# A GLU in five passes, Newton steps on GpSimd, and residual rows asked for ahead in a one-core YOCO decoder step

## The chip, the cores and the metric

The kernel runs on one core of one Trainium2 chip. The metric is the device time of one execution in microseconds; the median of three runs of the kernel before is 2706.2 us (2705.61 to 2708.99).

The core has TensorE (PE: matmuls and transposes into PSUM), VectorE (DVE) and ScalarE (ACT) for elementwise work, GpSimd (POOL), and SyncE (SP), whose queue issues nearly all DMAs here. Each engine takes its instructions in order.

## What is computed

A prompt of 1024 tokens and a sample batch of 8 x 8 tokens go through two layers of width 1024. Layer 0 is an S5 state-space mixer with a gated output (GLU) and a convolutional feed-forward network (FFN); layer 1 is differential attention and another FFN. What the change touches, in the reference's words:

```python
z = jax.nn.gelu(y)
gl = z @ w_glu                                   # 1024 -> 2048
out = gl[..., :D_MODEL] * jax.nn.sigmoid(gl[..., D_MODEL:])
x = x + rmsnorm(out, a_post_g)                   # end of the GLU: post norm and residual
h = rmsnorm(x, f_pre_g) @ w_up                   # FFN, up: 1024 -> 5632
f_out = (gelu(gate) * val) @ w_down              # after a 3-tap convolution; down: 2816 -> 1024
x = x + rmsnorm(f_out, f_post_g)                 # end of each FFN
```

Layer 1's attention ends in the same way: `x = x + rmsnorm(o @ w_o, b_post_g)`, and its FFN follows.

## The kernel before

Tokens lie in nine tiles: eight of 128 prompt tokens (0 to 7) and one of 64 sample tokens (number 8, NTT). Activations that a matmul reads stand transposed in SBUF as a rounded part `xh` and a remainder `xl`; a product is three matmuls (`mm3`, L805 to L807), for the sample tile two (L979, L980).

**GLU** (`glu`). The 2048 output columns are done in four passes `q`, each with 256 value columns and their 256 gate columns, over all nine tiles in `ORDER_U`. For each pass `glu_units(q)` loads four weight units of 512 KB and splits them into two parts (ScalarE L788, VectorE L789). A tile's pass is 24 matmuls of 512 columns (`tok_mm`), a sigmoid on ScalarE (L1042) and a product on VectorE (L1043) into 256 columns of the tile's row buffer `ao[tt]`. In the last pass each tile is finished by `tail.add`.

**Tails.** `tail_a` loads the residual rows (L845, into one of two buffers `xr`), takes the sum of squares on ScalarE (`square_sum`, L820), multiplies by the post gain (VectorE, L849), turns the mean square into 1/rms (`rstd_from`: two set-up instructions and three Newton steps of two 128x1 instructions each, L126 and L130), adds the residual (L852) and stores the rows (L853). `tail_n` does the norm of the next layer in the same way (L862). `tail_b` transposes the result (TensorE L868) and splits it into `xh` and `xl` (L140 on ScalarE, L141 on VectorE). `Combos.pair` does so for the tile pairs (0,3), (1,4), (2,5), and forms differences (L909 to L912) for a Strassen-like product in the up-projection. `Tail` keeps tiles that are normed but not yet transposed in a list; beyond `lag` of them the oldest is transposed. `lag` is 2 in the GLU and 1 in the output projection.

**Output projection** (`o_proj`). Column half 1 of the nine tiles is done in `ORDER_O`; the five tiles of `EARLY` (NTT, 0, 3, 1, 4), whose other half was computed during attention, are finished there. The four of `LATE` (2, 5, 6, 7) only give half 1 to DRAM (`yod`), with its share of the sum of squares (`part`), and are finished in a pass of their own over half 0.

**FFN.** `ffn_up` loops over 22 column pairs; each ends in a store of a gated row block to DRAM (`gd`, L1191). `ffn_down` takes the 22 blocks in chunks, adds partial products in `acc` (L1404), and calls `done(tt)` for each tile after the last chunk; in layer 1 that is `tail_a` alone, whose result is the kernel's output. A sample tile's two halves are first added through a buffer `xr` (L1370, L1371).

**Buffers.** `slot(tag)` hands out shared buffers: 14 of `acc` (row buffers, gains, combos), 5 of `gr` (512 columns), 2 of `xr`; weights come into 2 buffers `raw` and are split into 11 rotating ones. A planner orders the instructions of all engines for the whole program by priority (program order) and its own model of durations; on the chip each engine then keeps that order.

Of the kernel before, what the change touches and what calls it, by code (L numbers as in the profile page):

```python
# [10 lines left out]
F32 = mybir.dt.float32  # L11
# [62 lines left out]
def trunk_kernel(ctx, tc, I, O):  # L74
# [7 lines left out]
    def nm(s):  # L82
        uid[0] += 1
        return f"{s}_{uid[0]}"
# [23 lines left out]
    def flat(t, n=512):  # L108
        return t[:, 0:n]

    def rstd_from(pool, ss, n, parts, tag, n_mean=D, bufs=None, pre=None):


        kw = {"bufs": bufs} if bufs else {}
        v = pool.tile([P, n], F32, tag=tag + "v", name=nm("rv"), **kw)
        s = pool.tile([P, n], F32, tag=tag + "s", name=nm("rs"), **kw)
        r = pool.tile([P, n], F32, tag=tag + "r", name=nm("rr"), **kw)
        p = slice(0, parts)
        if pre is None:
            V.tensor_scalar(v[p], ss, -0.5 / n_mean, -0.5 * EPS, op0=ALU.mult, op1=ALU.add)  # L120
        else:
            V.scalar_tensor_tensor(v[p], ss, -0.5 / n_mean, pre, op0=ALU.mult, op1=ALU.add)
        V.tensor_scalar(r[p].bitcast(I32), v[p].bitcast(I32), -0.5, RSQ_MAGIC, op0=ALU.mult, op1=ALU.add)
        for _ in range(3):
            if n == 1:
                V.scalar_tensor_tensor(s[p], r[p], r[p], v[p], op0=ALU.mult, op1=ALU.mult)  # L126
            else:
                V.tensor_tensor(s[p], r[p], r[p], ALU.mult)
                V.tensor_tensor(s[p], s[p], v[p], ALU.mult)
            V.scalar_tensor_tensor(r[p], s[p], 1.5, r[p], op0=ALU.add, op1=ALU.mult)  # L130
        return r
# [677 lines left out]
    def tokens(tt):  # L809
        return (tt * P, P) if tt < NTT else (SEQ, TS)  # L810
# [12 lines left out]
    def rms_rstd(t, n):  # L823
        return rstd_from(pools["ph"], square_sum(t, n), 1, n, "n1", bufs=4)

    sums = {}

    def part(y, tt, post, cs):
# [8 lines left out]
            V.tensor_scalar(p, ss, -0.5 / D, -0.5 * EPS, op0=ALU.mult, op1=ALU.add)  # L837
        V.tensor_tensor(y, y, post[0:n, cs], ALU.mult)

    def tail_a(y, tt, post, xsrc, xdst, last=False, rest=slice(0, D)):  # L840


        t0, n = tokens(tt)
        xr = slot("xr")
        nc.sync.dma_start(xr[0:n], xsrc(tt))  # L845
        halves = (slice(512, D), slice(0, 512)) if last else (slice(0, D),)
        ss = square_sum(y[:, rest], n)
        for hs in halves if last else (rest,):
            V.tensor_tensor(y[:, hs], y[:, hs], post[0:n, hs], ALU.mult)  # L849
        r = rstd_from(pools["ph"], ss, 1, n, "n1", bufs=4, pre=sums.pop(tt, None))  # L850
# [4 lines left out]
    def tail_n(y, tt, gain=None):  # L855

        n = tokens(tt)[1]
        r = rms_rstd(y, n)
# [59 lines left out]
    class Tail:  # L918
# [6 lines left out]
        def add(self, y, tt, *a, **kw):  # L925
            tail_a(y, tt, *a, **kw)
            self.norm()
            self.n.append((y, tt))
            if len(self.q) > self.lag:
                self.pop()  # L930

        def norm(self):
            for a in self.n:
                tail_n(*a, self.gain)
            self.q += self.n
            self.n = []

        def pop(self):
# [74 lines left out]
    def glu(ws):  # L1013

        zt = slot("acc")[0:TS, 0:D]
        zv = zt.rearrange("r (b g c) -> r b g c", g=8, c=16)
        for u in range(3):
            for j in range(min(3, 8 - 3 * u)):
                zs = zsd.rearrange("(b u) r w -> u r b w", u=3)[u, 32 * j : 32 * j + NB]
                nc.sync.dma_start(zv[:, :, 3 * u + j], zs.rearrange("s b (t c) -> (s t) b c", c=16))  # L1020
        post = row_bcast(I["a_post_g"][0])
        tail.gain = row_bcast(I["f_pre_g"][0])
        ao = {}
        for q in range(4):
            if q:
                ws = glu_units(q)
            qs_ = slice(q * 256, (q + 1) * 256)
            for tt in ORDER_U:
                n = tokens(tt)[1]
                if q == 0:  # L1030
                    ao[tt] = slot("acc")
                    if tt == ORDER_U[4]:
                        tail_b(zt, NTT)
                        xsx = sample_pair()
# [6 lines left out]
                sg = slot("gr")  # L1041
                A.activation(sg[0:n, 0:256], g[:, 256:512], AF.Sigmoid)  # L1042
                V.tensor_tensor(ao[tt][0:n, qs_], g[:, 0:256], sg[0:n, 0:256], ALU.mult)  # L1043
                if q == 3:
                    if tt == 0:
                        tail.combos = Combos()
                    y = ao[tt][0:n, 0:D]
                    tail.add(y, tt, post, x_in, x_scr(x1d))
            if q == 0:
                conv_params(0)  # L1050
                lam_column(cpool)
        tail.norm()
# [305 lines left out]
            self.upto(1)  # L1358

    def ffn_down(dn, i, xsrc, xdst, norm):  # L1360
        acc = {}
        post = [None]
        nch = len(dn.plan)

        def done(tt):
            n = tokens(tt)[1]
            y = acc[tt][0:n, 0:D]
            if n < P:
                u = slot("xr")
                A.copy(u[0:n], acc[tt][n : 2 * n, 0:D])  # L1370
                V.tensor_tensor(y, y, u[0:n], ALU.add)  # L1371
            if norm:
                tail.add(y, tt, post[0], xsrc, xdst)
            else:
                tail_a(y, tt, post[0], xsrc, xdst, tt == NTT - 1)

        def plain(k, c, tt):
            kind, f0, nf = dn.plan[c]
# [93 lines left out]
        for k, (c, tt) in enumerate(dn.steps):  # L1472
            kind, f0, nf = dn.plan[c]
            if c == nch - 1 and post[0] is None:
                post[0] = row_bcast(I["f_post_g"][i])
            if kind == "p":
                dn.upto(k + 2)
                plain(k, c, tt)
# [486 lines left out]
    def o_proj():  # L1965
# [7 lines left out]
        for half, tts in ((1, ORDER_O), (0, LATE)):  # L1973
# [4 lines left out]
            for tt in tts:  # L1978
# [15 lines left out]
                else:  # L1994
                    fold_sample(yh, ps)
                if end:
                    tail.add(y, tt, post, x_scr(x2d), x_scr(x3d), rest=hs)
                else:
                    part(yh, tt, post, hs)
                    nc.sync.dma_start(yod[t0 : t0 + n], yh)  # L2000
                    tail.norm()
                    tail.pop()
# [2 lines left out]
    dtile = lambda name, shape: dpool.tile(shape, F32, tag=name, name=name)  # L2005
    x2d = dtile("x2d", [T, D])
    gd = dtile("gd", [NF, P, TG])
    x3d = dtile("x3d", [T, D])
    kd = dtile("kd", [T, D])
    vd = dtile("vd", [T, D])  # L2010
# [59 lines left out]
```

## Time and profile before

| | |
|---|---|
| median of three runs | 2706.2 us (2705.61 to 2708.99) |
| the profiled execution | 2703.74 us, span 2701.9 us |
| TensorE busy | 2499.0 us |
| VectorE busy | 1966.6 us |
| ScalarE busy | 1266.0 us |
| GpSimd busy | 666.8 us |
| mean granted TensorE clock | 0.974 |

Busy times are sums over the whole span. TensorE's work is spread over stages that each have a limit of their own; where its row in the span's slices is below 9, another engine or a transfer sets the pace. "Granted clock" is the share of TensorE's full speed that the throttle left it in a stretch.

### The profile page before, as it was taken

The numbers are of one execution on the slowest core, as the hardware profiler recorded it, in microseconds if no ns is written. First come the engines' busy times: TensorE is split into PE (matmuls) and PEld (weight loads), VectorE is DVE, ScalarE is ACT, GpSimd is POOL, SyncE is SP. The second block draws the span as 40 slices with busy tenths as digits, with TensorE's granted clock in tenths as the row PEclk, the third lists the DMA queues.
The fourth block names the chain that finished last, engine by engine and source line by source line (L and its number), as shares of the span: only waits on it lengthen the run. The fifth ranks groups of instructions, "written<-read, shape, count | busy, mean of one in ns | idle before, by whom it ended". The sixth has DMA issues, their size and how long they took to land.

```text
span 2701.9 us, 39378 instructions
## 1 busy us (share of the span) xinstructions
PE 2499.0 (92%) x14234; PEld 2201.1 (81%) x14234; DVE 1966.6 (73%) x3743; ACT 1266.0 (47%) x2499; POOL 666.8 (25%) x943
## 2 busy tenths in 40 slices
PE   3879997999999989999999799989899999999996
PEld 2767886999999967778777688877799999997774
DVE  7993349677777789985222688876877777778998
ACT  6762224444444453344322577764544444454432
POOL 3220000111222375501201322110021111137661
PEclk9999998999999999999999899999899999999998
DMA  5432322222222243444656333325322222233324
GB/s 144 104 96 79 93 68 89 65 74 73 74 73 74 88 123 89 117 133 169 213 164 205 88 94 94 95 90 190 109 73 74 73 74 74 78 98 110 100 87 148
DMA packets 258791, 280.73 MB, mean 104 GB/s; under 512 B 41836, under 2 KB 205988, under 8 KB 258596
## 3 DMA queue, kind: packets, MB, share of 16 engines
q1 hardware_dynamic: 254852, 266.99, 32.0%
q0 software_dynamic: 3232, 10.29, 1.7%
q8 instruction: 113, 1.85, 0.3%
q10 hardware_dynamic: 512, 0.92, 0.1%
q14 instruction: 82, 0.67, 0.1%
HBM read 189.91 MB, written 68.58 MB: 96 GB/s over the span
## 4 chain that ended last, share of the span: by engine, by line
PE 67%; DVE 17%; DMA 5%; ACT 5%; issue 4%; POOL 2%; SPq 0%; DVEq 0%; POOLq 0%; ACTq 0%
PE mm L805 19%; PE mm L806 19%; PE mm L807 19%; DVE acc L1404 2%; PE mm L1393 2%; DVE xT_lo L141 2%; DMA gr<-gd 1%; DVE S L1866 1%; ACT S L1870 1%; DVE xT_hi L141 1%; PE tr L868 1%; POOL xr L1285 1%; DVE wst L141 1%; PE mm L1894 1%; DMA raw<-in_w_down_dram 1%
## 5 line engine op out<-in xcount | busy, mean ns | idle before, releaser
L805 PE MATMUL mm<-xT_hi,whi 128*128 128x320 f32 (+1 forms) x1408 | 459.0, 327 | 4.2 <-ACT xT_hi L140 2.4
L806 PE MATMUL mm<-xT_lo,whi 128*128 128x384 f32 (+1 forms) x1408 | 457.1, 325 | 1.5 <-DVE xT_lo L141 1.5
L807 PE MATMUL mm<-xT_hi,wlo 128*128 128x384 f32 (+1 forms) x1408 | 456.1, 325 | 0.0
L1182 POOL COPY cvo<-acc 128x2 f32<-128x2 f32 x88 | 107.3, 1219 | 733.6 <-ACT acc L1165 733.6
L805 PEld LDWEIGHTS mm<-xT_hi,whi 128*128 128x128 f32 x1408 | 265.7, 189 | 9.2 <-DVE acc L1148 4.8
L806 PEld LDWEIGHTS mm<-xT_lo,whi 128*128 128x128 f32 x1408 | 266.3, 189 | 2.4 <-DVE xT_lo L141 2.3
L807 PEld LDWEIGHTS mm<-xT_hi,wlo 128*128 128x128 f32 x1408 | 266.1, 189 | 0.8
L805 PE MATMUL mm<-whi,xT_hi 128*128 128x512 f32 x608 | 242.3, 403 | 4.2 <-ACT whi L788 4.2
L806 PE MATMUL mm<-wlo,xT_hi 128*128 128x512 f32 x608 | 241.1, 397 | 0.0
L807 PE MATMUL mm<-whi,xT_lo 128*128 128x512 f32 x608 | 240.9, 398 | 0.0
L1179 DVE SCALAR_TENSOR_TENSOR acc<-acc,cpar,acc 128x1104 f32<-128x1104 f32 x176 | 238.9, 1378 | 0.4 <-ACT acc L1177 0.2
L141 DVE TENSOR_TENSOR wlo<-raw,whi 128x1024 fp32r<-128x1024 f32 x88 | 107.7, 1224 | 175.4 <-PE mm L806 161.5
L140 ACT CAST whi<-raw 128x1024 fp32r<-128x1024 f32 x88 | 92.5, 1052 | 251.5 <-PE mm L807 238.0
L1404 DVE TENSOR_TENSOR acc<-mm,acc 128x512 f32<-128x512 f32 x279 | 184.3, 679 | 10.2 <-PE mm L807 9.8
L805 PE MATMUL mm<-acc,whi 128*128 128x384 f32 x528 | 180.5, 342 | 0.9 <-DVE acc L1139 0.6
L806 PE MATMUL mm<-acc,whi 128*128 128x384 f32 x528 | 180.2, 341 | 0.0
L807 PE MATMUL mm<-acc,wlo 128*128 128x384 f32 x528 | 179.8, 341 | 0.0
L805 PEld LDWEIGHTS mm<-whi,xT_hi 128*128 128x128 f32 x608 | 115.2, 190 | 34.7 <-ACT whi L788 4.4
L807 PEld LDWEIGHTS mm<-whi,xT_lo 128*128 128x128 f32 x608 | 114.4, 188 | 27.9 <-issue 0.8
L806 PEld LDWEIGHTS mm<-wlo,xT_hi 128*128 128x128 f32 x608 | 114.4, 188 | 26.9 <-issue 0.4
L1177 ACT ACTIVATE acc<-acc,cpar 128x1104 f32<-128x1104 f32 x88 | 115.5, 1313 | 29.0 <-DVE acc L1148 21.7
L141 DVE TENSOR_TENSOR wlo<-xr,whi 128x1024 fp32r<-128x1024 f32 x88 | 107.6, 1223 | 19.9 <-PE mm L806 13.4
(568 smaller groups left out, 6201.6 us busy)
## 6 DMA issues: line engine op xcount, KB each, us to landing
raw<-in_w_up_dram SPq DMA_DIRECT2D x88, 512.0 KB
gd<-acc SPq DMA_DIRECT2D x44, 552.0 KB
raw<-in_w_down_dram SPq DMA_DIRECT2D x44, 512.0 KB
gr<-gd SPq DMA_DIRECT2D x80, 256.0 KB
raw<-in_glu_w_dram SPq DMA_DIRECT2D x32, 256.0 KB
acc<-in_cache_k_dram SPq DMA_DIRECT2D x16, 512.0 KB
acc<-in_cache_v_dram SPq DMA_DIRECT2D x16, 512.0 KB
xj<-in_x_prompt_dram SPq DMA_DIRECT2D x8, 512.0 KB
```

What stands on the lines that cost most here:

```text
L140: A.copy(hi_ap, ps_ap)
L141: V.tensor_tensor(lo_ap, ps_ap, hi_ap.bitcast(F32), ALU.subtract)
L805: PE.matmul(out, lh, rh, start=start, stop=False, **kw)
L806: PE.matmul(out, lh, rl, start=False, stop=False, **kw)
L807: PE.matmul(out, ll, rh, start=False, stop=stop, **kw)
L868: PE.transpose(ps[:, c * n : (c + 1) * n], y[:, c * P : (c + 1) * P], ident[0:n, 0:n])
L1177: A.activation(hc, hb[:, 2 : 2 + TG], AF.Identity, bias=cp[:, ft, 3:4], scale=cp[:, ft, 2:3])
L1179: V.scalar_tensor_tensor(hc, hb[:, tap : tap + TG], cp[:, ft, tap : tap + 1], hc, op0=ALU.mult, op1=ALU.add)
L1182: GP.tensor_copy(co[:, 0:2], hb[:, SEQ : SEQ + 2])
L1285: GP.tensor_tensor(v[n], v[dif[n][0]], v[dif[n][1]], ALU.subtract)
L1393: PE.matmul(pa[h], lt, wt[:, h * 512 : (h + 1) * 512], start=st and j == 0, stop=sp and j == len(seq) - 1)
L1404: V.tensor_tensor(a, ps, a, ALU.add)
```

## The change

- **Five passes.** The GLU runs quarter 0 and quarter 1 over all tiles, quarter 2 over EARLY, quarter 3 over all in `ORDER_O` (which finishes EARLY), then quarter 2 over LATE (which finishes LATE), with quarter 2's weights loaded a second time. Only EARLY tiles keep row buffers throughout; a LATE tile's quarters 0, 1 and 3 go to a DRAM buffer `aod` (in the free half of the sigmoid's `gr` buffer) and are loaded back in two pieces before the last pass. Every quarter but the last adds to the sum of squares and is multiplied by the gain at once (`part`).
- **GpSimd.** With `aside`, `rstd_from` issues its six Newton instructions on GpSimd, for the EARLY tiles of the GLU and of the output projection, in both norms.
- **Residual rows.** In layer 1's `ffn_down` four tiles' residual rows are asked for at the beginning of the last chunk, alternately into `raw` and `xr` buffers, and each `done` asks for those of the tile four places on. The sample tile's halves are added through two `gr` buffers in place of one `xr`, in both FFNs.

```diff
-    def rstd_from(pool, ss, n, parts, tag, n_mean=D, bufs=None, pre=None):
+    def rstd_from(pool, ss, n, parts, tag, n_mean=D, bufs=None, pre=None, aside=False):
...
         for _ in range(3):
+            if aside:
+                GP.tensor_scalar(s[p], r[p], r[p], v[p], op0=ALU.mult, op1=ALU.mult)
+                GP.tensor_scalar(r[p], s[p], 1.5, r[p], op0=ALU.add, op1=ALU.mult)
+                continue
...
-    def tail_a(y, tt, post, xsrc, xdst, last=False, rest=slice(0, D)):
+    def tail_a(y, tt, post, xsrc, xdst, last=False, rest=slice(0, D), aside=False, xr=None):
...
-        xr = slot("xr")
-        nc.sync.dma_start(xr[0:n], xsrc(tt))
+        if xr is None:
+            xr = slot("xr")
+            nc.sync.dma_start(xr[0:n], xsrc(tt))
...
-        for q in range(4):
-            if q:
+        for q, tts, end in ((0, ORDER_U, ()), (1, ORDER_U, ()), (2, EARLY, ()), (3, ORDER_O, EARLY), (2, LATE, LATE)):
+            if q or end:
                 ws = glu_units(q)
             qs_ = slice(q * 256, (q + 1) * 256)
-            for tt in ORDER_U:
-                n = tokens(tt)[1]
-                if q == 0:
+            for tt in tts:
+                t0, n = tokens(tt)
+                if tt in EARLY and q == 0 or tt in LATE and end is LATE:
                     ao[tt] = slot("acc")
...
+                if end is LATE:
+                    for cs in (slice(0, 512), slice(768, D)):
+                        nc.sync.dma_start(ao[tt][:, cs], aod[t0 : t0 + n, cs])
...
-                V.tensor_tensor(ao[tt][0:n, qs_], g[:, 0:256], sg[0:n, 0:256], ALU.mult)
-                if q == 3:
+                yq = ao[tt][0:n, qs_] if tt in ao else sg[:, 256:512]
+                V.tensor_tensor(yq, g[:, 0:256], sg[:, 0:256], ALU.mult)
+                if tt in end:
                     if tt == 0:
                         tail.combos = Combos()
-                    y = ao[tt][0:n, 0:D]
-                    tail.add(y, tt, post, x_in, x_scr(x1d))
+                    tail.add(ao[tt][0:n, 0:D], tt, post, x_in, x_scr(x1d), rest=qs_, aside=tt in EARLY)
+                else:
+                    part(yq, tt, post, qs_)
+                    if tt in LATE:
+                        nc.sync.dma_start(aod[t0 : t0 + n, qs_], yq)
+                        tail.norm()
+                        tail.pop()
...
+        def fetch(j):
+
+            if not norm and j <= NTT:
+                tt = ORDER[j]
+                r = slot("xr") if j % 2 else pools["w"].tile([P, 1024], F32, tag="raw", name=nm("raw"), bufs=2)
+                nc.sync.dma_start(r[0 : tokens(tt)[1]], xsrc(tt))
+                res[tt] = r
...
-                u = slot("xr")
-                A.copy(u[0:n], acc[tt][n : 2 * n, 0:D])
-                V.tensor_tensor(y, y, u[0:n], ALU.add)
+                for h in range(2):
+                    hs = slice(512 * h, 512 * h + 512)
+                    u = slot("gr")
+                    A.copy(u[0:n], acc[tt][n : 2 * n, hs])
+                    V.tensor_tensor(y[:, hs], y[:, hs], u[0:n], ALU.add)
...
-                tail_a(y, tt, post[0], xsrc, xdst, tt == NTT - 1)
+                tail_a(y, tt, post[0], xsrc, xdst, tt == NTT - 1, xr=res.pop(tt))
+                fetch(ORDER.index(tt) + 4)
...
                 post[0] = row_bcast(I["f_post_g"][i])
+                for j in range(4):
+                    fetch(j)
...
-                    tail.add(y, tt, post, x_scr(x2d), x_scr(x3d), rest=hs)
+                    tail.add(y, tt, post, x_scr(x2d), x_scr(x3d), rest=hs, aside=tt in EARLY)
```

## Rows read from the trace of the kernel before

**Rows 1.** The page's head and its first part: span and instructions, then busy time, share of the span and instructions of each engine.

```profile
span 2701.9 us, 39378 instructions
PE 2499.0 (92%) x14234; PEld 2201.1 (81%) x14234; DVE 1966.6 (73%) x3743; ACT 1266.0 (47%) x2499; POOL 666.8 (25%) x943
```

**Rows 2.** Windows of the GLU: its third pass, most of its fourth, and the stretch after its last matmul. Columns: stretch, its length, busy us (and instructions) of PE, PEld, DVE, ACT, POOL, granted clock, share of the DMA engines, GB/s.

```profile
320.00:368.35 48.35, 48.35 (x210) 38.92 (x209) 9.15 (x14) 8.17 (x14) 0.00 (x0) 1.00 0.13 44
384.40:425.90 41.50, 41.50 (x196) 33.71 (x195) 38.19 (x123) 19.38 (x39) 0.00 (x0) 1.00 0.37 127
425.90:482.00 56.10, 37.42 (x182) 32.58 (x182) 49.87 (x124) 26.32 (x50) 1.58 (x4) 0.76 0.27 85
```

**Rows 3.** The timeline of TensorE at the end of the GLU: start, duration, instruction, and in brackets the idle time before it and what ended it.

```profile
425.69 0.40 PE L807 MATMUL mm<-whi,xT_lo 128*128 128x512 f32 x1
...
441.91 1.09 PE L868 MATMUL tr<-ident,gr 128*128 128x128 f32 x4 [4.28 <-DVE rr L123]
```

**Rows 4.** Groups of VectorE's instructions from 384.4 to 477 us: busy us, mean ns of one, idle time before.

```profile
L852 DVE SCALAR_TENSOR_TENSOR acc<-acc,rr,xr 128x1024 f32<-128x1024 f32 x8 | 10.2, 1278 | 0.0
L862 DVE SCALAR_TENSOR_TENSOR acc<-acc,rr,acc 128x1024 f32<-128x1024 f32 x8 | 10.2, 1277 | 0.0
...
L849 DVE TENSOR_TENSOR acc<-acc,acc 128x1024 f32<-128x1024 f32 x8 | 9.8, 1224 | 1.8 <-ACT gr L820 1.7
L126 DVE SCALAR_TENSOR_TENSOR rs<-rr,rv 128x1 f32<-128x1 f32 x48 | 9.4, 213 | 0.2
L130 DVE SCALAR_TENSOR_TENSOR rr<-rs,rr 128x1 f32<-128x1 f32 x48 | 6.7, 153 | 0.3
L141 DVE TENSOR_TENSOR wlo<-raw,whi 128x1024 fp32r<-128x1024 f32 x3 | 3.7, 1221 | 1.3 <-ACT whi L140 1.2
```

**Rows 5.** Timelines: the first store of a gated row block in layer 0 (SP's queue), the last matmul of the output projection (TensorE), and the first store of a gated row block in layer 1. The GLU's last matmul is the first row of rows 3.

```profile
500.03 0.34 SPq L1191 DMA_DIRECT2D gd<-acc  x1
...
1912.49 0.39 PE L807 MATMUL mm<-whi,xT_lo 128*128 128x512 f32 x1
...
1967.19 0.34 SPq L1191 DMA_DIRECT2D gd<-acc  x1
```

**Rows 6.** Groups of TensorE's transposes after the GLU's last matmul (425.9 to 482 us, three rows) and around and after that of the output projection (1908 to 1950 us, two rows), and, from the chain of waits, twelve transposes in a row at full clock (start, duration).

```profile
L868 PE MATMUL tr<-ident,acc 128*128 128x128 f32 x36 | 6.5, 325 | 4.4 <-DVE xT_lo L141 2.9 <-DVE acc L141 1.5
L868 PE MATMUL tr<-ident,gr 128*128 128x128 f32 x32 | 6.2, 336 | 10.0 <-DVE rr L123 4.3 <-DVE gr L909 2.4 <-DVE acc L141 1.9
L868 PE MATMUL tr<-ident,acc 64*128 64x64 f32 x8 | 0.9, 231 | 1.6 <-DVE acc L862 1.6
...
L868 PE MATMUL tr<-ident,acc 128*128 128x128 f32 x28 | 5.5, 358 | 8.8 <-DVE rs L126 5.7 <-DVE acc L862 3.1
L868 PE MATMUL tr<-ident,gr 128*128 128x128 f32 x16 | 2.4, 274 | 0.0
...
415.32 1.31 PE tr L868 x12
```

**Rows 7.** Windows of the output projection, columns as in rows 2: the EARLY tiles' tails, the change of weights between its two passes, and the stretch in which its matmuls end and the up-projection begins.

```profile
1857.00:1905.00 48.00, 48.00 (x237) 39.00 (x237) 42.44 (x120) 26.17 (x58) 0.00 (x0) 1.00 0.53 172
1880.00:1890.00 10.00, 10.00 (x53) 8.26 (x52) 9.07 (x17) 6.94 (x14) 0.00 (x0) 1.00 0.78 255
1905.00:1945.00 40.00, 28.69 (x138) 24.75 (x137) 39.00 (x113) 21.22 (x43) 1.34 (x4) 0.80 0.39 129
```

**Rows 8.** GpSimd's small copies in the up-projection and VectorE beside them: the group of 88 copies from the page, timelines of GpSimd at 503 and 520 us, of VectorE at 520 us, and of VectorE's Newton steps alone at 386 us.

```profile
L1182 POOL COPY cvo<-acc 128x2 f32<-128x2 f32 x88 | 107.3, 1219 | 733.6 <-ACT acc L1165 733.6
...
503.74 0.18 POOL L1182 COPY cvo<-acc 128x2 f32<-128x2 f32 x1 [3.68 <-ACT acc L1165]
...
520.44 3.62 POOL L1182 COPY cvo<-acc 128x2 f32<-128x2 f32 x1 [16.03 <-ACT acc L1165]
...
520.44 1.30 DVE L1190 TENSOR_TENSOR acc<-acc,acc 128x1104 f32<-128x1104 f32 x1
521.66 2.36 DVE L141 TENSOR_TENSOR wlo<-xr,whi 128x1024 fp32r<-128x1024 f32 x2
523.93 0.56 DVE L1142 TENSOR_TENSOR acc<-mm,acc 128x384 f32<-128x384 f32 x1
...
386.34 0.22 DVE L126 SCALAR_TENSOR_TENSOR rs<-rr,rv 128x1 f32<-128x1 f32 x1
...
386.79 0.22 DVE L126 SCALAR_TENSOR_TENSOR rs<-rr,rv 128x1 f32<-128x1 f32 x1
```

**Rows 9.** The timeline of VectorE at the end of the kernel: the last residual additions, with the idle time before each and what ended it.

```profile
2684.14 1.28 DVE L852 SCALAR_TENSOR_TENSOR acc<-acc,rr,xr 128x1024 f32<-128x1024 f32 x1
...
2686.32 1.28 DVE L852 SCALAR_TENSOR_TENSOR acc<-acc,rr,xr 128x1024 f32<-128x1024 f32 x1 [0.18 <-DMA xr<-x3d]
...
2689.97 1.28 DVE L852 SCALAR_TENSOR_TENSOR acc<-acc,rr,xr 128x1024 f32<-128x1024 f32 x1 [1.25 <-DMA xr<-x3d]
2693.34 1.28 DVE L852 SCALAR_TENSOR_TENSOR acc<-acc,rr,xr 128x1024 f32<-128x1024 f32 x1 [2.08 <-DMA xr<-x3d]
2697.05 1.42 DVE L852 SCALAR_TENSOR_TENSOR acc<-acc,rr,xr 128x512 f32<-128x512 f32 x2 [2.43 <-DMA xr<-x3d]
```

**Rows 10.** The chain of waits at the end of the kernel: two residual loads on it (start, duration).

```profile
2685.84 4.11 DMA xr<-x3d
...
2691.68 5.28 DMA xr<-x3d
```

More of the change, by code (lines that the diff above doesn't have):

```diff
@@ L821, in square_sum @@
         return ss[0:n]
-    def rms_rstd(t, n):
-        return rstd_from(pools["ph"], square_sum(t, n), 1, n, "n1", bufs=4)
     sums = {}
@@ L849, in tail_a @@
             V.tensor_tensor(y[:, hs], y[:, hs], post[0:n, hs], ALU.mult)
-        r = rstd_from(pools["ph"], ss, 1, n, "n1", bufs=4, pre=sums.pop(tt, None))
+        r = rstd_from(pools["ph"], ss, 1, n, "n1", bufs=4, pre=sums.pop(tt, None), aside=aside)
         for hs in halves:
@@ L853, in tail_a, with tail_n @@
             nc.sync.dma_start(xdst(tt)[:, hs], y[:, hs])
-    def tail_n(y, tt, gain=None):
+    def tail_n(y, tt, aside, gain=None):
         n = tokens(tt)[1]
-        r = rms_rstd(y, n)
+        r = rstd_from(pools["ph"], square_sum(y, n), 1, n, "n1", bufs=4, aside=aside)
         if gain is None:
@@ L923, in __init__, with add @@
             self.n, self.q, self.combos, self.gain, self.lag = [], [], None, None, 2
-        def add(self, y, tt, *a, **kw):
-            tail_a(y, tt, *a, **kw)
+        def add(self, y, tt, *a, aside=False, **kw):
+            tail_a(y, tt, *a, aside=aside, **kw)
             self.norm()
-            self.n.append((y, tt))
+            self.n.append((y, tt, aside))
             if len(self.q) > self.lag:
@@ L934, in norm @@
                 tail_n(*a, self.gain)
-            self.q += self.n
+            self.q += [a[:2] for a in self.n]
             self.n = []
@@ L1023, in glu @@
         ao = {}
-        for q in range(4):
-            if q:
+        for q, tts, end in ((0, ORDER_U, ()), (1, ORDER_U, ()), (2, EARLY, ()), (3, ORDER_O, EARLY), (2, LATE, LATE)):
+            if q or end:
                 ws = glu_units(q)
             qs_ = slice(q * 256, (q + 1) * 256)
-            for tt in ORDER_U:
-                n = tokens(tt)[1]
-                if q == 0:
+            for tt in tts:
+                t0, n = tokens(tt)
+                if tt in EARLY and q == 0 or tt in LATE and end is LATE:
                     ao[tt] = slot("acc")
-                    if tt == ORDER_U[4]:
-                        tail_b(zt, NTT)
-                        xsx = sample_pair()
+                if end is LATE:
+                    for cs in (slice(0, 512), slice(768, D)):
+                        nc.sync.dma_start(ao[tt][:, cs], aod[t0 : t0 + n, cs])
+                if q == 0 and tt == ORDER_U[4]:
+                    tail_b(zt, NTT)
+                    xsx = sample_pair()
                 ps = tok_mm(tt, ws, None if n == P else xsx)
@@ L1040, in glu @@
                     g = ps
-                sg = slot("gr")
-                A.activation(sg[0:n, 0:256], g[:, 256:512], AF.Sigmoid)
-                V.tensor_tensor(ao[tt][0:n, qs_], g[:, 0:256], sg[0:n, 0:256], ALU.mult)
-                if q == 3:
+                sg = slot("gr")[0:n]
+                A.activation(sg[:, 0:256], g[:, 256:512], AF.Sigmoid)
+                yq = ao[tt][0:n, qs_] if tt in ao else sg[:, 256:512]
+                V.tensor_tensor(yq, g[:, 0:256], sg[:, 0:256], ALU.mult)
+                if tt in end:
                     if tt == 0:
                         tail.combos = Combos()
-                    y = ao[tt][0:n, 0:D]
-                    tail.add(y, tt, post, x_in, x_scr(x1d))
+                    tail.add(ao[tt][0:n, 0:D], tt, post, x_in, x_scr(x1d), rest=qs_, aside=tt in EARLY)
[5 more added lines that the diff above has]
+                        tail.pop()
             if q == 0:
@@ L1360, in ffn_down @@
     def ffn_down(dn, i, xsrc, xdst, norm):
-        acc = {}
+        acc, res = {}, {}
         post = [None]
         nch = len(dn.plan)
+        def fetch(j):
[4 more added lines that the diff above has]
+                res[tt] = r
         def done(tt):
@@ L2007, in trunk_kernel @@
     gd = dtile("gd", [NF, P, TG])
+    aod = dtile("aod", [SEQ, D])
     x3d = dtile("x3d", [T, D])
```

## The prediction

> **What bounds the kernel now.** I read first the page's totals, then the stretch around the end of the GLU in windows, then its instructions, then the same stretch of the output projection, and last the end of the kernel. TensorE is busy 2499.0 of 2701.9 us [rows 1], so time is to be had only where TensorE waits. A whole GLU pass is full: 48.35 us busy of 48.35 [rows 2], and nothing that is added beside it costs anything as long as VectorE (9.15 us busy there) has room. The last pass is another matter. All nine tiles are finished in it, so all their tails (square sum, Newton steps, residual, second norm, transposes) fall in one place: VectorE is busy 38.19 of 41.50 us while the pass runs and 49.87 of 56.10 us after its end, TensorE only 37.42 of those 56.10, at a mean granted clock of 0.76 [rows 2]. The matmuls of the GLU end at 425.69 and the next things in TensorE's queue are single groups of transposes with gaps before them, the longest 4.28 us, each ended by VectorE [rows 3]. What VectorE does there is nine each of the post multiplication (1224 ns), the residual (1278 ns) and the norm (1277 ns), and 54 pairs of Newton steps (213 and 153 ns; eight tiles' 48 in the row) [rows 4]. So the boundary between GLU and up-projection is bound by VectorE, and so is the end of the kernel, where its last four residual additions wait 1.25 + 2.08 + 2.43 us and, before them, 0.18 us for residual rows from DRAM [rows 9].
>
> **Part 1, the GLU in five passes.** The matmuls stay the same: 24 per full tile and pass, the third quarter only cut into two visits. What moves is the tails of the five EARLY tiles: they start one short pass earlier, beside the whole last-quarter pass (48.35 us [rows 2]), and then the LATE tiles have a pass of their own of 4 x 24 matmuls. One pass has 8 x 24 + 16 = 208 matmuls, 48.35/208 = 0.23 us each, so the LATE pass lasts 4 x 24 x 0.23 = 22 us.
>
> The nearest measure is in this very kernel: the output projection already ends as the new GLU will, with nine tiles in one pass and four LATE ones in a pass of their own, followed by the same up-projection. From the last projection matmul to the first store of a gated row it takes 1967.19 - 1912.49 = 54.7 us; the GLU takes 500.03 - 425.69 = 74.3 us [rows 5]. The difference is 19.6 us. Not all of it is gain: in the output projection 44 transposes are left after the last matmul, in the GLU 76 [rows 6], and the 32 that move ahead must still be run, at 1.31/12 = 0.109 us [rows 6], 3.5 us. That leaves 19.6 - 3.5 = 16 us.
>
> What is added: four weight units of the third quarter are loaded and split again, 4 x 1.22 us of VectorE [rows 4] and as many casts on ScalarE, and 8 DMAs on SP; the output projection changes weights at the same point and TensorE stays busy 10.00 of 10.00 us over it [rows 7], so I cost it at nothing (uncovered, one unit is some 2.3 us). For 27 tile visits, a square sum and a 256-wide multiplication replace the 1024-wide ones of the last pass; beside a full pass with VectorE at 9.15 of 48.35 us they are hidden. Twelve stores of 128 KB and eight loads of LATE rows go through SP, which the weight loads share; their like in the output projection runs with TensorE full [rows 7]. One difference counts against the analogue: the GLU lets two normed tiles lie before it transposes the next (the output projection one), so the pair of tiles 2 and 5 comes after the first up-projection matmuls; I put 0 to 4 us on it, and take 1.
>
> **Part 2, Newton steps on GpSimd.** For the five EARLY tiles of both stages, 2 x 3 x 2 = 12 instructions a tile leave VectorE, 60 a stage. Alone a pair takes VectorE 386.79 - 386.34 = 0.45 us [rows 8], among other work only its 0.2 us of throughput: 30 pairs free 6 to 13.5 us of VectorE. In the output projection these steps lie in 1857 to 1905, where TensorE is at 48.00 of 48.00; the waits come after, in 1905 to 1945 (TensorE 28.69, VectorE 39.00 of 40) [rows 7], where only LATE tiles are left. So relief there is worth little.
>
> On GpSimd the trace has no 128x1 arithmetic. The nearest row is the 128x2 copy: 0.18 us with VectorE idle, 1219 ns in the mean of 88, and 3.62 us at 520.44, where it ends as VectorE passes from three instructions with two SBUF inputs (start 520.44 and 521.66) to one that reads PSUM (523.93) [rows 8]. So six steps take 1.1 us at the least and 7.3 at the mean of that row. I take some 0.6 us each, nearer the low end, since beside the EARLY tails VectorE often reads PSUM and idles when it waits for GpSimd itself: 60 x 0.6 = 36 us, which fits in 48. A chain of 3.6 us in place of one that VectorE now drags through other work is about even. The plan of the instructions' order is made with assumed durations, though, and each late chain holds VectorE's in-order queue at the residual addition: I allow 0.5 us of spill in each stage, with bounds of -3 and +8 us for each.
>
> The page "SBUF — State Buffer" of the Trainium skill (Who interferes with whom) says that a VectorE instruction with two SBUF inputs and a GpSimd one that reads SBUF exclude each other, the second waiting for the first to end, in either direction. The rows agree for GpSimd's side [rows 8]; that GpSimd also holds up VectorE no row here isolates, and by the rule the 60 steps would take back about 60 x 0.18 = 11 us of VectorE a stage, more than the low end of what they free; this is part of rival (b).
>
> **Part 3, the end.** Before, each tile's residual is asked for when the tile is done, behind the previous tile's store, with two places; a load takes 4.11 to 5.28 us on the chain of waits [rows 10]. With four places asked for ahead, the loads of the last tiles start after the addition four tiles before instead of two. VectorE's idle time at the end is 0.18 + 1.25 + 2.08 + 2.43 = 5.94 us [rows 9], and that is the most that can go: the rest of the stretch VectorE is full. What is late next is VectorE's own sum. Against it: the last load waits for the addition at 2684.14 [rows 9] and needs 4.11 us or more, so it lands at some 2690, about when it is wanted (0 to 1.5 us lost, I take 0.5); four loads in SP's queue ahead of the next gated rows' load may delay the latter (0 to 5 us; I take 0.5, since they are asked for before that load is due). The sample's sum in two halves adds an instruction each to ScalarE and VectorE, not counted. End: -5.9 + 1 = -5 us.
>
> **Sum.** -16 + 1 (lag) + 2 x 0.5 (GpSimd) - 5 = -19 us against the profiled execution of 2703.74 us (span 2701.9 and 1.84 around it): 2684.7. The median of the three runs, 2706.2, lies 2.5 us above that execution, so I forecast 2687 us.
>
> **Rivals.** (a) GpSimd becomes the bound, and the kernel gets slower. If a step takes the copy's mean of 1.22 us [rows 8], 60 steps take 73 us, where the EARLY tiles have 48 until the LATE pass; the buffers that the third and fourth LATE tile need come from the fourth and fifth EARLY, so TensorE stands some 20 us in each stage: +40 - 20 = +20, 2726 us. It decides from 48/60 = 0.8 us a step on. For it: VectorE is at 42.44 of 48.00 us there [rows 7], mostly with two SBUF inputs. Against it: VectorE waits for those very steps, and then they run at 0.2 us. 10 in 100 (with its milder form, around 2715).
> (b) The boundary stays: VectorE's queue is only shifted, since with GpSimd's late chains the EARLY tails spill 5 to 6 us into the LATE pass in both stages, which is VectorE's 39.00 of 40 us again: -19 + 11 = -8, 2698 us. 15 in 100; for it speaks that the planner makes one order and in-order queues keep it; and GpSimd's steps may hold up VectorE in turn (60 x 0.18 = 11 us a stage at the copy's shortest row [rows 8]); against it that VectorE has 48.00 - 42.44 = 5.6 us free there [rows 7] even before the steps leave it.
> (c) The residual loads get in the way of the gated rows' loads and the end gains nothing: -14, 2692 us. 12 in 100.
> (d) The gains are lost in a new order elsewhere, since the whole program is planned anew: 2706 us. 5 in 100.
>
> **How the numbers follow.** The forecast has 58 in 100, with 2676 to 2696 as its own range: at the low end GpSimd's -3 in each stage, no loss by the lag, and the whole 5.9 of the end; at the high end the lag's 4 us and some 3 us in each stage. The range wanted for 8 in 10 reaches over (c) and most of (b): 2676 to 2703. What a measurement of this kernel can tell from no change is 0.2%, 5.4 us: faster is below 2700.8. The forecast, (c) and two thirds of (b) are faster: 0.58 + 0.12 + 0.10 = 0.80; same 0.10 ((d) and the rest of (b)); slower 0.10.
>
> **What would show it.** Right: first gated store some 55 us after the GLU's last matmul, TensorE full through five passes; GpSimd's steps at 0.2 to 0.8 us; no wait above 1 us before the last additions. Wrong: TensorE waiting for transposes inside the last-quarter pass with GpSimd busy before them (a); the boundary still above 65 us (b); SP's waits ahead of the gated rows' loads in the last chunk (c).

## The result and the profile after

| | before | after |
|---|---|---|
| median | 2705.9 us (2703.14 to 2708.99, 4 runs) | 2688.72 us (2687.25 to 2690.95, 4 runs) |
| profiled execution, span | 2703.74, 2701.9 | 2689.85, 2686.9 |
| ratio of the times | | 0.9937, 95% interval 0.992 to 0.9954 |

The change saves 17.2 us; 19 were forecast, and the time lies 1.7 us from the forecast. The sum came out better than its parts, as the stages show. I cut the span at eight events that both traces have and subtract (us):

| stage, ended by | before | after | difference |
|---|---|---|---|
| GLU and first column pair: first gated store, layer 0 | 500.0 | 482.3 | -17.7 |
| up-projection 0: last gated store | 473.0 | 467.7 | -5.4 |
| down-projection 0, keys, values: head 0's query weight asked for | 502.1 | 505.0 | +2.9 |
| attention: last `w_o` load ahead of the output projection | 294.9 | 300.2 | +5.3 |
| output projection: its last matmul | 142.5 | 147.0 | +4.5 |
| its tails: first gated store, layer 1 | 54.7 | 56.6 | +1.9 |
| up-projection 1: last gated store | 469.1 | 469.1 | 0 |
| down-projection 1: end | 265.6 | 259.0 | -6.6 |

Of these the first is what the five passes were forecast to do, and the last is the residual rows. Three more, of 3 to 5 us each, lie where the diff changes nothing, but for the sum of the sample tile's halves in the first down-projection.

The page's head after, to set beside [rows 1]: the same matmuls, 60 VectorE instructions fewer net, 120 more on GpSimd.

```profile
span 2686.9 us, 39636 instructions
PE 2491.3 (93%) x14234; PEld 2196.3 (82%) x14234; DVE 1964.9 (73%) x3683; ACT 1272.3 (47%) x2559; POOL 655.4 (24%) x1063
```

Windows of the end of the GLU after (stretch, length, busy us of PE, PEld, DVE, ACT, POOL, clock, DMA), against [rows 2]: 

```profile
382.00:431.00 49.00, 48.18 (x235) 38.91 (x234) 40.30 (x102) 22.11 (x54) 9.73 (x25) 1.00 0.48 164
431.00:482.00 51.00, 39.63 (x242) 38.22 (x241) 44.07 (x85) 26.02 (x42) 5.96 (x12) 0.90 0.23 73
```

The timelines after of TensorE (the GLU's last matmul, the longest gap behind it, the output projection's last matmul) and of SP (the first gated stores of both layers), against [rows 3] and [rows 5]:

```profile
430.42 0.39 PE L811 MATMUL mm<-whi,xT_lo 128*128 128x512 f32 x1
...
444.58 0.66 PE L870 MATMUL tr<-ident,gr 128*128 128x128 f32 x2 [9.72 <-DVE gr L911]
...
482.32 0.34 SPq L1204 DMA_DIRECT2D gd<-acc  x1
...
1902.21 0.39 PE L811 MATMUL mm<-whi,xT_lo 128*128 128x512 f32 x1
...
1958.76 0.34 SPq L1204 DMA_DIRECT2D gd<-acc  x1
```

The last matmul comes 4.7 us later (more tails run beside the passes; the prediction had 3.5 us for their 32 transposes, and TensorE stands still for 0.8), and the first gated store 482.32 - 430.42 = 51.9 us behind it, where it was 74.3. VectorE is still the one that TensorE waits for, now chiefly in one gap of 9.72 us, but with 44.07 busy us behind the last matmul where it had 49.87.

The group of VectorE's last residual additions, first before (2681 to 2702 us), then after (2666 to 2687 us); the last column is the idle time ahead of them, which is the sum of the waits in [rows 9]:

```profile
L852 DVE SCALAR_TENSOR_TENSOR acc<-acc,rr,xr 128x1024 f32<-128x1024 f32 (+1 forms) x7 | 7.8, 1129 | 5.9 <-DMA xr<-x3d 5.9
```

```profile
L854 DVE SCALAR_TENSOR_TENSOR acc<-acc,rr,raw 128x1024 f32<-128x1024 f32 (+1 forms) x5 | 5.2, 1067 | 0.0
L854 DVE SCALAR_TENSOR_TENSOR acc<-acc,rr,xr 128x1024 f32<-128x1024 f32 x3 | 3.8, 1277 | 0.0
```

No wait for a residual row is left. The end is best read when it is cut at TensorE's last matmul, 2676.84 us before and 2670.99 after (windows, columns as above; first before, then after):

```profile
2676.84:2701.90 25.06, 0.39 (x2) 0.00 (x0) 15.57 (x47) 1.40 (x4) 0.00 (x0) 0.56 0.69 251
```

```profile
2670.99:2686.90 15.91, 0.40 (x2) 0.00 (x0) 11.63 (x34) 1.15 (x2) 0.00 (x0) 0.67 0.71 264
```

This stretch is 9.2 us shorter: VectorE is idle for 5.2 us less in it, and 3.9 us of its work now lie ahead of the last matmul. Part of that is paid back there. A gated rows' load stands in SP's queue behind a store and a residual load, and TensorE waits for ScalarE to split those rows; this is SP, then TensorE, after:

```profile
2643.59 0.51 SPq L855 DMA_DIRECT2D out_y_sample_dram<-acc  x1
2644.19 0.53 SPq L1383 DMA_DIRECT2D raw<-x3d  x1
2644.78 0.59 SPq L1355 DMA_DIRECT2D gr<-gd  x1
...
2649.77 0.50 PE L809 MATMUL mm<-wst,acc 128*128 128x512 f32 x1 [1.11 <-ACT acc L144]
```

From the last gated store to the last matmul it takes 243.1 us, where it took 240.6 before.

### The profile page after: what moved, and what is told of

It is laid out like the page before. It is cut to its first block, busy times and chain, and to the rows that moved or that the text cites. A ratio compares the mean times of both kernels' runs of the same rounds, so it can differ in the third digit from the quotient of the medians.

```text
span 2686.9 us, 39636 instructions
## 1 busy us (share of the span) xinstructions
PE 2491.3 (93%) x14234; PEld 2196.3 (82%) x14234; DVE 1964.9 (73%) x3683; ACT 1272.3 (47%) x2559; POOL 655.4 (24%) x1063
## 4 chain that ended last, share of the span: by engine, by line
PE 58%; DVE 14%; DMA 4%; issue 3%; ACT 3%; POOL 2%; SPq 0%; DVEq 0%; POOLq 0%; ACTq 0%
PE mm L809 17%; PE mm L811 17%; PE mm L810 17%; DVE acc L1428 2%; DMA gr<-gd 2%; DVE S L1892 2%; DVE xT_lo L145 1%; PE mm L1417 1%; ACT S L1896 1%; DVE acc L854 1%; DVE wst L145 1%; DVE xT_hi L145 1%; DVE S L1906 1%; PE mm L1920 1%; PE tr L870 1%
## 5 line engine op out<-in xcount | busy, mean ns | idle before, releaser
L809 PE MATMUL mm<-xT_hi,whi 128*128 128x384 f32 (+1 forms) x1408 | 456.2, 325 | 2.0 <-ACT acc L1146 1.7
L1195 POOL COPY cvo<-acc 128x2 f32<-128x2 f32 x88 | 53.4, 607 | 815.8 <-ACT acc L1178 815.8
L809 PE MATMUL mm<-whi,xT_hi 128*128 128x512 f32 x608 | 243.1, 403 | 4.9 <-ACT whi L792 4.8
L1190 ACT ACTIVATE acc<-acc,cpar 128x1104 f32<-128x1104 f32 x88 | 114.1, 1311 | 18.1 <-DVE acc L1161 11.9
```

The source lines that it names most:

```text
L809: PE.matmul(out, lh, rh, start=start, stop=False, **kw)
L1190: A.activation(hc, hb[:, 2 : 2 + TG], AF.Identity, bias=cp[:, ft, 3:4], scale=cp[:, ft, 2:3])
L1195: GP.tensor_copy(co[:, 0:2], hb[:, SEQ : SEQ + 2])
```

## The experiments

Each median stands beside runs of the kernel before on the same chip: 2708.12 us (22 runs) in the first four, 2707.13 (17) in the next four, 2705.88 (11) in the last. One trace is one execution: the span of a kernel varies by some 10 us between its runs, so a stage is believed when several traces agree.

**One part at a time.** First the five passes alone: the changed kernel without its two other parts.

```diff
-tail.add(ao[tt][0:n, 0:D], tt, post, x_in, x_scr(x1d), rest=qs_, aside=tt in EARLY)
+tail.add(ao[tt][0:n, 0:D], tt, post, x_in, x_scr(x1d), rest=qs_)
-tail.add(y, tt, post, x_scr(x2d), x_scr(x3d), rest=hs, aside=tt in EARLY)
+tail.add(y, tt, post, x_scr(x2d), x_scr(x3d), rest=hs)
 # and no fetch() in ffn_down
```

> The GLU's five passes alone: all Newton steps on VectorE, residual rows asked for as before. Theory (the passes carry the gain, as the output projection's boundary said): first gated store about 52 to 55 us after the GLU's last matmul and some 15 to 18 us earlier than before, end at 2686 to 2692 us. Rival 1 (the gain at this boundary is GpSimd's, which takes the EARLY tiles' Newton steps off a full VectorE): the boundary stays above 60 us and the time above 2697 us.

Measured 2703.35 us, ratio 0.9989 (0.9979 to 1.0). The boundary moved as forecast (first gated store at 484.4 us in its trace, 54.2 behind the last matmul), so it is the passes that shorten it and not GpSimd's steps. Still little was left: the time is 11 us above the theory's range. Its trace, taken in the fastest of its 11 runs (2695.74 us), loses 4.0 us in attention and 10.2 in layer 1: 59.3 + 474.7 us from the output projection's last matmul to the last gated store, against 54.7 + 469.1 before.

Then the kernel before with GpSimd in the output projection alone (`aside=tt in EARLY` in `o_proj`, nothing else).

> The kernel before with one edit: the EARLY tiles' Newton steps of the output projection on GpSimd. Theory after the trace of the changed kernel (the output projection lost some 5 us there, 3 of them with TensorE waiting inside its first pass): 2708 to 2712 us. Rival (the steps are hidden there, as forecast; what was lost came from elsewhere): 2704 to 2707 us.

Measured 2709.43 us, 1.0007 (0.9998 to 1.0016): nothing that can be told apart. In its trace, though, the output projection and its tails take 204.9 us, where they took 197.2.

The kernel before with the residual rows alone (`fetch` and the sample's sum in two halves).

> The kernel before with one edit: residual rows of the last FFN asked for ahead in four places (and the sample's halves added through two gr buffers). Theory: the waits of 5.9 us before the last additions go, 2699 to 2701 us. Rival (c) of the prediction, that the loads get in the way of the gated rows' loads: 2704 to 2707 us.

Measured 2698.2 us, 0.9965 (0.9953 to 0.9978): 9.9 us faster, twice the 5 of the forecast. Its last stage is 257.6 us against 265.6, 8.0 shorter.

The changed kernel without GpSimd in the output projection.

> The changed kernel with the output projection's Newton steps back on VectorE. Theory (GpSimd costs 5 us there): 2682 to 2685 us. Rival (hidden): 2688 to 2690 us, as the changed kernel.

Measured 2695.54 us, 0.9954 (0.994 to 0.9968), some 4 to 7 us slower than the changed kernel (the two intervals overlap), though fewer steps ran on GpSimd; theory and rival both lie lower. Its trace shows where, in two SP rows each, the first and the last gated store of layer 1, first this kernel, then the changed one:

```profile
1957.38 0.34 SPq L1204 DMA_DIRECT2D gd<-acc  x1
...
2433.86 0.33 SPq L1204 DMA_DIRECT2D gd<-acc  x1
```

```profile
2427.88 0.33 SPq L1204 DMA_DIRECT2D gd<-acc  x1
```

It starts the up-projection 1.4 us earlier than the changed kernel (1958.76 above) and ends it 6.0 later: 476.5 us for the 21 steps between, against 469.1. **The up-projection runs in one of two orders.** In TensorE's queue the four transposes of two column pairs stand as 3 + 1 in one and as 2 + 1 + 1 in the other; the first takes 43.9 us for two pairs, the second 44.7 once it has settled. The kernel before has the slow one in layer 0 and the fast one in layer 1, the changed kernel the fast one in both, and the five passes alone, as well as this kernel, the slow one in layer 1. That is the 5.4 us of layer 0 in the table, and most of what these two kernels lose.

**What makes the slow order slow?** In it the product of the last 320 columns is late in every pair from the middle of the loop on, eleven times in layer 0 of the kernel before. TensorE waits for an eviction that VectorE's queue has behind a weight split. These are two pairs; 711.75 - 711.22 = 0.53 us from start to start in the one and 734.11 - 733.74 = 0.37 in the other, where 0.17 is usual, and the next matmul comes after 0.25, where 0.15 is usual:

```profile
711.22 0.34 PE L807 MATMUL mm<-acc,wlo 128*128 128x384 f32 x1
711.75 0.41 PE L805 MATMUL mm<-xT_hi,whi 128*128 128x320 f32 x1 [0.20 <-DVE acc L1148]
712.00 0.31 PE L806 MATMUL mm<-xT_lo,whi 128*128 128x320 f32 x1
...
733.74 0.33 PE L807 MATMUL mm<-xT_hi,wlo 128*128 128x384 f32 x1
734.11 0.41 PE L805 MATMUL mm<-xT_hi,whi 128*128 128x320 f32 x1
734.36 0.31 PE L806 MATMUL mm<-xT_lo,whi 128*128 128x320 f32 x1
```

VectorE beside the second, split and eviction:

```profile
732.36 1.23 DVE L141 TENSOR_TENSOR wlo<-raw,whi 128x1024 fp32r<-128x1024 f32 x1 [6.00 <-PE mm L806]
733.50 0.55 DVE L1148 TENSOR_TENSOR acc<-mm,acc 128x384 f32<-128x384 f32 x1
```

The eleven together are some 4.2 of the 5.4 us. The fast loops have no such start.

My theory was that the product needs the very PSUM bank that is being evicted, so I gave it others, in four kernels.

```diff
 def rest(f, s):
-    ps = psum()
+    ps = psum_t()
```

> The kernel before, with one thing changed: in the up-projection of both FFNs the product of the last 320 columns goes to the three PSUM banks of the transposes and no longer to the five that the Strassen-like products share. Theory (the up-projection runs in one of two orders; in the slower one TensorE waits about 0.4 us a column pair for VectorE's eviction of a product, which is queued behind a weight split, because the next product needs that very bank): without the shared bank no wait, 21.9 us or less a pair in both layers; layer 0, at 22.4 a pair before, gains 5 to 9 us, layer 1, at 21.9, nothing: 2698 to 2703 us. Rival (the order itself, with its scattered transposes, costs the time, not the bank): this kernel's plan has the scattered order in both layers, so layer 1 also goes to 22.35 a pair, some 2708 + 8 = 2716 us.

> The changed kernel with the same change of PSUM banks. Its two up-projections ran at 21.9 us a pair before this. Theory: no eviction wait in either layer, 2685 to 2690 us, the same as the changed kernel or a little less, though the plan now has the scattered order of transposes in both layers. Rival: the scattered order costs 0.42 us in each of 2 x 22 pairs or most of them: 2700 to 2707 us.

> The changed kernel with the same change of PSUM banks, and the Newton steps of the output projection on VectorE again (those of the GLU stay on GpSimd). Theory: with equal up-projections what is left is GpSimd's cost in the output projection, 3 to 5 us: that much faster than the changed kernel with the same banks, 2681 to 2686 us. Rival (the Newton steps on GpSimd do help the output projection, as the changed kernel without them was 7 us slower): 4 to 8 us slower than it, 2693 to 2697 us.

> The changed kernel with the same change of PSUM banks and no Newton step on GpSimd at all: five passes and the residual rows alone. Theory (GpSimd's steps cost or give about nothing in the GLU, since the first gated store came at 482.3 and 487.4 us with them and at 484.4 without): within 2 us of the kernel that keeps them in the GLU alone, 2681 to 2688 us. Rival (they relieve VectorE there): 4 us or more slower than that one, 2686 to 2692 us.

Measured 2719.95 us (1.0047, 1.0034 to 1.006), 2721.61 (1.0052, 1.0039 to 1.0064), 2713.7 (1.0032, 1.002 to 1.0043) and 2713.73 (1.0024, 1.0014 to 1.0033). All are slower than before, 17 to 32 us above the theory's ranges and 4 to 22 above the rival's. The product no longer waits for the eviction, but in 5 to 7 pairs of each loop it is still late, by 0.42 and 0.60 us from start to start, now for the weight split itself. This is the changed kernel with the new banks, layer 0:

```profile
835.77 0.41 PE L811 MATMUL tr<-xT_hi,wlo 128*128 128x320 f32 x1 [0.26 <-DVE wlo L145]
```

So the bank was not all that made the product late, and what it costs by itself is not shown: TensorE also waits in other places in these kernels (in that layer 3.0 us for GpSimd's copies ahead of the conv transposes, and 5.0 ahead of the down-projection, where the changed kernel has 3.8), and all eight loops take 475.2 to 476.9 us. The four share the transposes' banks with the tails as well; in the changed kernel the first gated store went from 482.3 to 489.6 us, in the kernel before from 500.0 to 498.7.

With these banks all loops are about equally long, so that the last three can be compared. Without GpSimd in the output projection the changed kernel is 7.9 us faster, more than the 3 to 5 of the theory; in the traces 8.4 us of it lie in the output projection and its tails (212.2 and 203.8). The last two differ by nothing in their medians: GpSimd in the GLU or not.

**The beginning of attention.** With the original banks, the kernels with five passes took 299 to 300 us for attention so far, those with four 293 to 296. In the changed kernel GpSimd's queue stands at head 0's value load, whose buffer lies where the last samples' rows are still being stored, and the weight and key work of head 0 is queued behind it (before, the same load waited 9.44 us). GpSimd's queue and two windows over all engines, after:

```profile
1455.97 0.89 POOL L1803 DMA_DIRECT2D kr<-kd  x1
1475.92 0.88 POOL L1787 DMA_DIRECT2D v<-vd  x1 [19.06 <-DMA od<-acc]
1476.82 1.91 POOL L1806 TENSOR_TENSOR qraw<-qraw,bpg 128x1024 f32<-128x1024 f32 x1
```

```profile
1460.00:1470.00 10.00, 4.72 (x104) 2.90 (x104) 6.75 (x46) 3.53 (x15) 0.00 (x0) 0.91 0.24 86
1470.00:1480.00 10.00, 0.14 (x1) 0.14 (x1) 0.00 (x0) 1.24 (x2) 2.91 (x3) 0.50 0.50 161
```

TensorE has 0.14 of 10 us after 4.72 in the 10 before, and its granted clock falls from 0.91 in the mean to 0.50, the lower of its two levels (1.2 GHz). The next four kernels keep the fast order in both layers. The first takes that buffer ahead of the others of head 0, so that it lies elsewhere:

```diff
 def prep(h):
+    if h == 0:
+        H["v"] = at([P, NTT, VD], "v0")
     raw = at([P, KT, P], "qraw")
```

> The changed kernel with one thing changed at the beginning of attention: head 0's buffer for the value rows is taken ahead of its weight buffers, so that it lies elsewhere and its load waits for two transfers instead of the last stores of the samples' rows (19.06 us of GpSimd's queue, TensorE 0.14 of 10 us in 1470 to 1480). Both up-projections keep the order of the changed kernel (transposes in threes and ones). Theory (attention gave back 4 to 5 us of what the GLU gained, through this wait): the load goes out some 9 us or more earlier, 4 to 5 us faster than the changed kernel, 2683 to 2686 us. Rival (what follows on TensorE is late for another reason, such as the key rows or the weight's split, or another buffer of head 0 now has the wait): 2687 to 2691 us.

Measured 2675.7 us (2671.18 to 2679.06), 0.9894 (0.988 to 0.9908), against 0.9937 for the changed kernel: some 12 us, more than twice what the theory gave. The load now goes straight out:

```profile
1457.27 0.89 POOL L1806 DMA_DIRECT2D kr<-kd  x1
1458.15 0.89 POOL L1788 DMA_DIRECT2D v<-vd  x1
1461.81 1.90 POOL L1809 TENSOR_TENSOR qraw<-qraw,bpg 128x1024 f32<-128x1024 f32 x1 [2.77 <-DMA qraw<-in_w_q_dram]
```

```profile
1465.00:1475.00 10.00, 8.75 (x28) 6.49 (x29) 8.24 (x28) 3.54 (x8) 4.47 (x5) 0.66 0.33 71
```

Attention takes 290.4 us, 9.9 less than in the changed kernel, and 289.7 to 290.8 in the three kernels below. This is the fastest kernel of the study. Whether the kernel before would gain by the same line was not tried.

**GpSimd's steps, with the orders kept.** With the line above, only the first of the two norms on GpSimd:

```diff
 def tail_n(y, tt, aside, gain=None):
-    r = rstd_from(..., "n1", bufs=4, aside=aside)
+    r = rstd_from(..., "n1", bufs=4, aside=False)
```

> The kernel with head 0's value buffer taken first, and GpSimd's Newton steps only in the first of the two norms of each EARLY tile (30 steps a stage instead of 60; the second norm's go back to VectorE). Both up-projections keep their order. Theory (GpSimd's steps hold up the transposes in the output projection, TensorE at 9.56, 9.38 and 9.49 of 10 us there): 1 to 3 us faster than with both norms on GpSimd, 2681 to 2685 us. Rival (they relieve VectorE): 2 to 4 us slower than it.

The same with six iterations on GpSimd in place of three:

```diff
-for _ in range(3):
+for _ in range(6 if aside else 3):
```

> The kernel before this one (GpSimd in the first norm alone) with six Newton iterations in place of three wherever they run on GpSimd, which changes no result but doubles GpSimd's steps: at 0.62 + 0.27 us a pair (means of the changed kernel in the GLU) 5 tiles x 3 pairs x 0.89 = 13 us more of GpSimd in each stage, 2.7 us in each tile's chain. Both up-projections keep their order. Theory (VectorE's queue waits at each residual addition, partly covered): 2 to 6 us slower than with three, 2684 to 2690 us. Rival (all hidden beside the full pass): within 1.5 us. Rival (GpSimd becomes the bound): 15 us slower or more.

And the second kernel without GpSimd in the GLU:

> The kernel with GpSimd in the first norm alone, without GpSimd in the GLU (30 steps in the output projection are left). Both up-projections keep their order. Theory (in the GLU the steps cost or give nothing that can be seen, as their relief of VectorE and the longer chains even out): within 2 us of the kernel that has them in both stages. Rival (they relieve VectorE at the end of the GLU, where it is full): 3 to 6 us slower. Rival (they cost there as in the output projection): 1 to 3 us faster.

Measured 2678.61 us (0.99, 0.9886 to 0.9915), 2687.09 (0.9927, 0.9915 to 0.994) and 2680.15 (0.9903, 0.9889 to 0.9917). Half the steps back on VectorE is 2.9 us slower, within the two kernels' intervals, where the theory had 1 to 3 faster; GpSimd taken out of the GLU is 1.5 slower, as the theory had it. In the output projection the second norm's steps do hold TensorE up. These are windows that end some 22 us before its last matmul, first of the changed kernel, then of the one with the first norm alone:

```profile
1870.00:1880.00 10.00, 9.38 (x47) 7.30 (x46) 8.77 (x15) 4.56 (x10) 1.08 (x4) 1.00 0.57 190
```

```profile
1861.00:1871.00 10.00, 10.00 (x54) 8.22 (x52) 9.88 (x19) 6.95 (x14) 0.00 (x0) 1.00 0.67 217
```

But the tenths that TensorE loses there (1.6 us in 30 in the changed kernel, 1.2 in the fastest, none in the one with the first norm alone) are not seen in the time. That VectorE sets the pace right after may be why; no run tells. Doubling the steps costs 8.5 us, more than the 2 to 6 of the theory. VectorE's residual additions in the GLU wait 11.9 us for GpSimd in place of 5.9 (list of waits, 340 to 460 us, doubled first):

```profile
DVE acc L854 <- POOL rr L127: 11.9, 5, 5.2
```

```profile
DVE acc L854 <- POOL rr L127: 5.9, 5, 1.8
```

In the traces, though, only 1.3 us more lie in the GLU and 1.7 in the tails of the output projection; 7.1 of the 11 us between these two traces lie between the first up-projection and attention, where no such step runs, and there TensorE waits 3.5 us for the cached keys in place of 1.4. How much of the 8.5 is GpSimd's is open; 3 us are seen.

## Why the prediction was right, point by point

- **What bounds the boundary** was right. VectorE is the one that TensorE waits for there, before and after, and moving its work ahead of the last matmul shortens it.
- **Part 1** (-16 and +1 for the lag, so -15) was right in mechanism and size. The analogue gave a first store about 55 us after the last matmul; it came after 51.9, and after 51.9 to 55.7 in all seven traces below. In the traces of the seven kernels with five passes and the original banks it comes at 482.3 to 487.4 us, 484.7 in the mean, in the three with four passes at 498.8 to 500.2, 499.7: -15.0. What the lag cost in it no run tells. That TensorE would be full through all five passes holds within 0.8 us (48.18 of 49.00).
- **Part 2** (0.6 us a step, +0.5 us in each stage) was right that GpSimd would not be the bound, and too dear in the price of a step. These are the groups of the GLU (355 to 440 us), 60 steps in 25.2 us, 0.42 each:

```profile
L126 POOL TENSOR_SCALAR rs<-rr,rv 128x1 f32<-128x1 f32 (+1 forms) x30 | 17.0, 570 | 148.2 <-DVE rr L123 145.4 <-DVE rv L120 1.5
L127 POOL TENSOR_SCALAR rr<-rs,rr 128x1 f32<-128x1 f32 (+1 forms) x30 | 8.2, 279 | 1.6
```

  That is far from the 0.8 us at which rival (a) decides. Its cost of 0.5 us in the GLU lies below what the runs resolve: the steps on GpSimd or not made 0.0 and 1.5 us there. The 0.5 us in the output projection have no run behind them; see rival (b).
- **Part 3** (-5) had the right mechanism, and by the traces the size, but the sum was made up otherwise. The last stage takes 255.8 to 262.2 us in the ten traces with the rows asked for ahead, 259.7 in the mean, and 263.4 to 265.7 in the four without, 265.0: -5.3. Behind the last matmul 9 us go (15.3 to 16.1 us are left of 23.9 to 25.1). So the 5.94 us of waits were not the most that could go: VectorE's work there got less as well, which I had called full. Ahead of the last matmul the stage got longer, to 240.5 to 246.6 us from 239.4 to 240.6. The wait of TensorE for late gated rows, for which I had 0.5 us, is 1.0 to 1.9 in each of the ten traces and in none of the others; this is a mild form of rival (c). The residual rows alone were 9.9 us faster in the median and 8.0 in this stage of the trace; why more than in the other kernels is open.
- **Rival (b)** did not come in the GLU. The output projection and its tails, however, took 6.4 us longer than before in the trace after. Three pairs of kernels differ in GpSimd's steps there alone, and in each the two stages together are longer with them: 204.9 us against 197.2 (the kernel before), 203.5 against 201.1 (the changed kernel) and 212.2 against 203.8 (the new banks). That points at GpSimd, and at more than the 0.5 us of the sum, though each of these is a single trace. It is not shown to be the only cause: the fastest kernel has all steps on GpSimd and takes 197.9, its two kernels with half of them there 203.0 and 203.4, and without any such step the traces of the other kernels with the first banks give 199.4 to 203.0. What else sets this is open.
- **Rival (d)**, that a new plan moves time elsewhere, had 5 in 100 as a pure loss. It is what the forecast missed in kind: the plan gave 5.4 us in the first up-projection (its fast order), and a buffer's place took 5 us or more at the beginning of attention. These two cancel. The 6.4 us above and 2.9 between the first down-projection and attention remain, so that the stages without a gain of mine lose 9.2 us together. The total is near the forecast all the same, because the first and the last stage gave 24.3 us in these traces, where the sum had 20, and because the medians lie 2.2 us further apart than the two spans. That is luck in part.

So the time was met with the two main terms right, and with gains and losses of 5 us each that no step of mine had. The low end of the forecast's own range, 2676, is 2678 by its terms.

On the page "SBUF — State Buffer" of the Trainium skill (Who interferes with whom): GpSimd's side of it is seen again, VectorE's is not. A step takes 0.26 to 0.34 us with VectorE idle or nearly so and 1.38 beside a residual addition that starts while it runs (GpSimd's spans are rough):

```profile
366.48 1.38 POOL L126 TENSOR_SCALAR rs<-rr,rv 128x1 f32<-128x1 f32 x1
```

```profile
366.53 1.28 DVE L854 SCALAR_TENSOR_TENSOR acc<-acc,rr,xr 64x1024 f32<-64x1024 f32 x1 [1.82 <-POOL rr L127]
```

That addition takes its usual time: L854's mean in 355 to 440 us is 1282 ns with GpSimd's steps and 1282 in the kernel without them. The 11 us a stage that I had estimated for VectorE by that rule don't show.

## What to carry to other kernels

Where an engine's work piles up behind the last matmul of a stage, finish part of the tiles a pass earlier; a stage of the same kernel that already ends so is a good measure of what that gives. When a program is planned as a whole, no edit is local: compare stage by stage, and look at the order of loops and at where buffers fall before a gain or loss is put down to the edit. A wait at the head of an in-order queue for a buffer that belongs to the stage before costs more than it looks: moving one allocation gave two thirds of what the whole change had given.

## What had not been expected

Two orders of the same loop differ by 0.8 us in 44.7, while TensorE's windows of 20 us read 20.00 in the fast one and 19.80 to 20.00 in the slow one; only from start to start of single matmuls are the holes to be seen. And a GpSimd instruction on 128x1 values (the first of a step's pair, L126) ran in 0.34 us alone and in 1.38 beside VectorE, while VectorE's own instruction kept its 1.28. Nor did the prediction have it that residual rows asked for ahead take work of VectorE, and not its waits alone, from behind the last matmul.
